# Low-rank products and key norms on exact halves, with two raw weight tiles in place of three, in a hybrid decoder layer

## The chip, the cores and the metric

The kernel runs on one core of a Trainium2 chip. What is measured is the device time of one execution, in microseconds (us). A core has five engines that run side by side and meet through semaphores: TensorE (PE; its weight loads are listed as PEld), VectorE (DVE), ScalarE (ACT), GpSimd (POOL) and SyncE (SP). Here SP issues nearly all of the transfers between memory and the on-chip buffer, one after the other; an issue whose conditions aren't met holds up those behind it.

## The reference

One layer of a decoder with a residual stream x of 512 tokens and 2048 features, in float32. One input projection of the normed x feeds three mixers, whose outputs are joined, projected and added to x; a SwiGLU feed-forward part (FFN) with 5632 hidden features and a last norm follow. The change lies in the third mixer, RWKV-7, which has 16 heads of 64 features:

```python
logw = -softplus(-(w0 + tanh(wl) @ w2)) - 0.5
decay = exp(-exp(logw))
a = sigmoid(a0 + al @ a2)                    # the "rate"
kk = k * k_k
kk = kk / max(sqrt(sum(kk * kk, per head)), 1e-12)
k = k * (1 + (a - 1) * k_a)
# then, per head and token t, with a state S of 64 x 64:
#   S = S * decay_t + (S @ -kk_t) (kk_t a_t)^T + v_t k_t^T ;  y_t = S @ r_t
```

`wl` and `al` are low-rank features (96 wide) that come out of the input projection, as r, k and v do.

## The kernel before

**Products.** All large products run on exact halves: an fp32 matrix w is split into wh = fp32r(w) and wl = w − wh, and a product takes three passes, wh·xh, wh·xl and wl·xh (`dense_k`, L237), all added up in one PSUM bank. A weight tile is 128x1024 (eight blocks of 128x128): one transfer into a `raw` tile issued on SP (L226), the cast to `wh` on ACT (L230), the subtraction to `wl` on DVE (L231), then 24 matmuls on PE, each 512 columns wide. There are three raw tiles and two pairs of `wh`, `wl`. Weights of the next projection are asked for before the current one runs (`sequence`). A few small products run on plain fp32 operands, where a matmul is two instructions.

**Stages.** `load_x` loads x, splits it and computes the low-rank features (pd_l). Then come the projections of the mixers, in this order: gl, then k, r, v of eight RWKV pairs (two heads each, numbered 0 to 7), then q, k, v of the attention heads (qa, ka, va, qb and so on). The output projection and the FFN follow.

**RWKV steps of a pair**, written as Python generators that stand in lanes: `rates` makes z (decay, from w2 and wl) and pa (rate, from a2 and al), each one fp32 product of 512 columns; `prep` makes kn (sums of squared keys per head, a product with the block-ones constant `onesbd`), then two halves of the score blocks gr, each of which DVE masks; `inverse` and `join` invert the unit triangular blocks: linv goes out to memory (li), comes back as x, is solved in a row of small DVE operations (xt, xy), goes out as xi and comes back into linv with four transfers on SP, and then three groups of 32x32 products on PE (px, pt, po) finish it. `chain` is the recurrence over eight chunks of 64 tokens: z on PE, a copy zs on ACT, u on PE, copies uv on ACT, S on PE, an update of uv on DVE, then the next z. `post` makes vt, bon, var and g. In names like z3_6 the first number is the pair, the second the chunk; z3 alone is the decay product. All the steps of several pairs overlap.

**What sets the order.** After each dense matmul a planner, `pump`, lets those lanes take a step whose time has come. It counts time by the matmuls issued: n/2400 + 0.013 us for an fp32r product of n columns, twice n/1200 for an fp32 one (`mm`), and an estimate for each ACT and DVE instruction. `need(name)` runs lanes, without dense matmuls, until the step named is done: the eviction of a projection needs the tile of the pair before to be free (pd_v of pair hp needs step v of pair hp − 1, pd_r needs that of hp − 2), and each attention projection needs some step of pair 7. On every engine the instructions run in the order so written.

Of the kernel before, what the change touches and what calls it, by code (L numbers as in the profile page):

```python
# [14 lines left out]
P = 128  # L15
T = 512
# [31 lines left out]
CST = {}  # L48
_n = 0
for _name, _w in (  # L50
    ("ident", 128), ("onesbd", 128), ("ones", 128), ("centre", 128), ("mask", 128),
    ("eps", 1), ("gneps", 1), ("kneps", 1), ("knmin", 1),
):
    CST[_name] = _n
    _n += _w
# [33 lines left out]
class Kernel:  # L89
# [178 lines left out]
    def run(self):  # L268
        nc, tc = self.nc, self.tc
        with contextlib.ExitStack() as es:  # L270
            enter = es.enter_context
            nc.push_inst_callback(self.charge)
            es.callback(nc.pop_inst_callback)
            self.cp = enter(tc.tile_pool(name="cp", bufs=1))
            self.raw = enter(tc.tile_pool(name="raw", bufs=3))
            self.hl = enter(tc.tile_pool(name="hl", bufs=2))
            self.pools = {"raw": [self.raw], "hl": [self.hl]}
            self.xp = enter(tc.tile_pool(name="xp", bufs=KT))
            self.dp = enter(tc.tile_pool(name="dp", bufs=1, space=bass.MemoryType.DRAM))
            self.pd = enter(tc.tile_pool(name="pd", bufs=2, space=bass.MemoryType.PSUM))  # L280
            self.pm = enter(tc.tile_pool(name="pm", bufs=2, space=bass.MemoryType.PSUM))

            self.cols = self.cp.tile([P, NCOL], F32, name="cols")
            self.cc = self.cp.tile([P, NCST], F32, name="cc")
            nc.scalar.dma_start(out=self.cols, in_=self.i["cols"])
            nc.scalar.preload_act_table_set("natural_log_exp_and_others")
            mixer = enter(contextlib.ExitStack())
            self.py = mixer.enter_context(tc.tile_pool(name="py", bufs=1, space=bass.MemoryType.PSUM))
            self.pc = mixer.enter_context(tc.tile_pool(name="pc", bufs=3, space=bass.MemoryType.PSUM))
            self.lora_ps = self.load_x()  # L290
            items = self.mixer_items(mixer.enter_context)

            def mixers_end():
                mixer.close()
                self.ffn_pools(enter)
            self.mixers_end = mixers_end
            y = []
            items += self.wout_items(y)
            items += self.ffn_items(y)
            self.sequence(items)  # L300

    def load_x(self):
# [3 lines left out]
        with self.tc.tile_pool(name="sx", bufs=KT) as sx:  # L306
# [5 lines left out]
            for q in range(4):  # L312
                for e in range(4):
                    k = 4 * q + e
                    xk = sx.tile([P, T], F32, tag="x", name=f"x{k}", bufs=KT)
                    nc.sync.dma_start(out=xk, in_=self.i["xT"][:, k, :])
                    hi = self.xp.tile([P, T], F32R, tag="xh", name=f"xh{k}")
                    lo = self.xp.tile([P, T], F32R, tag="xl", name=f"xl{k}")
                    g = self.col("g_attn", k)
                    nc.scalar.activation(hi, xk, AF.Copy, scale=g)  # L320
                    nc.vector.scalar_tensor_tensor(out=lo, in0=xk, scalar=g, in1=hi.bitcast(F32),
                                                   op0=ALU.mult, op1=ALU.subtract)
                    self.xr.append((hi, lo))
                    xs.append(xk)
                    if e < 3:
                        src, m = srcs[e]
                        raw = self.raw.tile([P, 4 * m], F32, tag="raw", name=f"raw_l{e}_{q}")
                        nc.sync.dma_start(out=raw.rearrange("p (k m) -> p k m", m=m), in_=src[:, 4 * q:4 * q + 4, :])
                        w = slice(4 * q * m, 4 * (q + 1) * m)
                        if q:  # L330
                            nc.gpsimd.tensor_copy(out=his[e][:, w], in_=raw)
                        else:
                            nc.scalar.copy(out=his[e][:, w], in_=raw)
                        nc.vector.tensor_tensor(out=los[e][:, w], in0=raw, in1=his[e][:, w].bitcast(F32),
                                                op=ALU.subtract)
            nc.scalar.dma_start(out=self.cc, in_=self.i["cst"])
            ps = [p.tile([P, T], F32, tag=t, name=f"pd_l{j}")
                  for j, (p, t) in enumerate(((self.pd, "d"), (self.pd, "d"), (self.pm, "m")))]
            for k in range(KT):
# [38 lines left out]
    def shift_steps(self, f, ps, mu, name, m=P):  # L378

        nc = self.nc  # L380
        h = self.rp.tile([P, T + 8], F32, tag="h", name=f"h_{name}", bufs=2)
        nc.gpsimd.memset(h[:m, 7:8], 0.0)
        nc.vector.tensor_tensor(out=h[:m, 8:], in0=ps[:m, :], in1=self.rstd1[:m, :], op=ALU.mult)
        yield
# [16 lines left out]
    def mixer_items(self, enter):  # L401
# [6 lines left out]
        nc.vector.tensor_scalar(out=self.ol, in0=self.cols[:, c0:c0 + n], scalar1=-1.0, scalar2=1.0,  # L408
                                op0=ALU.mult, op1=ALU.add)

        self.wl = lp.tile([97, T], F32, name="wl")
        nc.gpsimd.memset(self.wl[96:97, :], 1.0)
        f = rp.tile([P, T], F32, tag="r", name="f_wl", bufs=2)
        self.shifted(f, self.lora_ps[0], ("mu_wl", 0), "wl", 96)
        th = nc.scalar.activation(self.wl[:96, :], f[:96, :], AF.Tanh)
        with tc.issue_after(th.ins):
            nc.scalar.preload_act_table_set("natural_log_exp_and_others")
        self.al = lp.tile([P, T], F32, name="al")
        self.shifted(self.al, self.lora_ps[1], ("mu_al", 0), "al", 96)
        self.gl = []  # L420
        items = []
        for j in range(2):
            def go(ps, j=j):
                f = rp.tile([P, T], F32, tag="r", name=f"f_gl{j}", bufs=2)
                self.shifted(f, ps, ("mu_gl", j), f"gl{j}")
                g = lp.tile([P, T], F32, name=f"sgl{j}")
                self.sigmoid(g, f)
                self.gl.append(g)
            if j:
                items.append(self.proj(1, "gl1", go, (self.pc, "c")))  # L430
            else:
# [47 lines left out]
    def rates(self, hp):  # L479
        nc, rp = self.nc, self.rp  # L480
        q = self.in_flight[hp]
        if hp and f"prep{hp - 1}" not in self.done:
            yield lambda: not (hp and f"prep{hp - 1}" not in self.done)
        yield 1.0 if hp else 15.0
        ch = slice(hp * P, (hp + 1) * P)
        w2 = rp.tile([97, P], F32, tag="w2", name=f"w2_{hp}", bufs=3)
        a2 = rp.tile([96, P], F32, tag="w2", name=f"a2_{hp}", bufs=3)
        nc.sync.dma_start(out=w2, in_=self.i["w2"][:, ch])
        nc.sync.dma_start(out=a2, in_=self.i["a2"][:, ch])

        ps = self.pm.tile([P, T], F32, tag="m", name=f"z{hp}")
        self.mm(ps, w2, self.wl)
        sg = rp.tile([P, NCH, 65], F32, tag="rn", name=f"sg{hp}")
        nc.gpsimd.memset(sg[:, :, 0:1], 0.0)

        pa = self.pm.tile([P, T], F32, tag="m", name=f"pa{hp}")
        self.mm(pa, a2, self.al[:96, :], start=True, stop=True)
        a = rp.tile([P, T], F32, tag="a", name=f"a{hp}")
        self.sigmoid(sg[:, :, 1:65], ps.rearrange("p (n c) -> p n c", c=C))
        self.sigmoid(a, pa, nbias=self.na0[:, hp:hp + 1])  # L500
# [14 lines left out]
    def prep(self, hp):  # L515
# [7 lines left out]
        rn = rp.tile([P, T], F32, tag="rn", name=f"rn{hp}")  # L523
        kk_g = self.col("k_k", hp)
        nc.scalar.activation(rn, k, AF.Square, scale=kk_g)
        yield
        ps = self.pm.tile([P, T], F32, tag="m", name=f"kn{hp}")
        self.mm(ps, self.cst("onesbd", P), rn, start=True, stop=True)
        kk = rp.tile([P, T], F32, tag="kk", name=f"kk{hp}")
        with self.tc.high_priority(self.lead):  # L530

# [95 lines left out]
        rkm = rp.tile([P, P], F32, tag="w2", name=f"rkm{hp}", bufs=3)  # L627
        nc.scalar.activation(rkm, self.cst("onesbd", P), AF.Copy, scale=self.col("r_k", hp))
# [136 lines left out]
    def post(self, q, py):  # L765
# [7 lines left out]
        self.mm(ps, self.cst("onesbd", P), sq, start=True, stop=True)  # L773
# [103 lines left out]
    def diff_head(self, h, q, vtag):  # L877
        nc, rp = self.nc, self.rp
        if "setup" not in self.done:
            yield lambda: not ("setup" not in self.done)  # L880
        bias = rp.tile([P, T], F32, tag="h", name=f"bias{h}", bufs=2)
# [79 lines left out]
    def swa_tile(self, i, q, kv):  # L961

        nc, rp = self.nc, self.rp
        bias = rp.tile([P, 2, 256], F32, tag="h", name=f"biasb{i}", bufs=2)
# [148 lines left out]
    def ffn_pools(self, enter):  # L1113
# [3 lines left out]
        self.pf = enter(tc.tile_pool(name="pf", bufs=4, space=bass.MemoryType.PSUM))  # L1117
        self.acc2 = self.fp.tile([P, T], F32, name="acc2", bufs=1)
        self.xr2 = []
        raw = enter(tc.tile_pool(name="raw2", bufs=3))  # L1120
        hl = enter(tc.tile_pool(name="hl2", bufs=1))
        self.pools = {"raw": [self.raw, raw], "hl": [self.hl, self.hl, hl]}

# [192 lines left out]
```

## Time and profile before

| | us |
|---|---|
| median of 3 runs (lowest, highest) | 2424.39 (2423.8, 2425.11) |
| the profiled execution, its span | 2425.95, 2424.2 |
| start: x and the low-rank products | 0 to 46.6 |
| mixers, with the first half of the output projection | 46.6 to 859.9 |
| second half of the output projection | 859.9 to 965 |
| FFN | 965 to 2388 |
| last norm and output | 2388 to 2424.2 |

The profile gives for every group of instructions its busy time, the mean length of one, and the idle time before it with what ended it. The chain of waits follows the work back from the last instruction and splits the span by what it waited for. A stretch of the timeline gives start, length, engine, line and operation; matmuls overlap, so that the distance between two starts, not the length, is what one costs. Windows give the busy time of each engine between two points of time, and then the clock that TensorE was granted, as a share of full speed.

### The profile page before, as it was taken

The page shows a single profiled execution, that of the slowest core. Times are in us where ns is not written, and L with a number is a line of the kernel's source. Part 1 is how long each engine was busy: PE and PEld are TensorE (multiplying, and loading weights), DVE is VectorE, ACT ScalarE, POOL GpSimd, SP SyncE. Part 2 cuts the span into 40 slices and gives each one's busy share as a digit, 9 for nine tenths or more (in the row PEclk, how much of TensorE's full clock was granted, in tenths as well). Part 3 has the DMA queues.
Part 4 walks back from the last instruction along what each step waited for, and adds up shares of the span by engine and source line. Part 5 has one row for each costly group of instructions (what it writes and reads, how often), then busy time and mean ns, then how long its engine had stood idle before and what let it go on. Part 6 is the DMA issues. An engine that isn't in the chain of part 4 may idle for free.

```text
span 2424.2 us, 30859 instructions
## 1 busy us (share of the span) xinstructions
PE 2398.7 (99%) x12328; PEld 1912.3 (79%) x12328; DVE 1185.3 (49%) x2129; ACT 806.4 (33%) x1375; POOL 100.0 (4%) x158
## 2 busy tenths in 40 slices
PE   8999999999999999999999999999999999999997
PEld 6777767777777788888888888888888888888887
DVE  7578778664555544343343434343434333343437
ACT  5445554544444433222222222222222222222124
POOL 3000000000000013000000000000000000000007
PEclk9999999999999999999999999999999999999999
DMA  5322222223225233233222223222222322222333
GB/s 176 100 85 73 84 77 85 79 87 97 92 79 165 87 133 99 95 100 96 96 96 96 96 99 100 97 96 96 96 96 99 101 96 96 96 96 96 99 101 132
DMA packets 103794, 240.05 MB, mean 99 GB/s; under 512 B 34906, under 2 KB 43746, under 8 KB 103650
## 3 DMA queue, kind: packets, MB, share of 16 engines
q1 hardware_dynamic: 98754, 231.39, 29.9%
q10 hardware_dynamic: 4896, 6.69, 0.8%
q8 instruction: 97, 1.59, 0.3%
q14 instruction: 47, 0.39, 0.0%
HBM read 227.55 MB, written 10.49 MB: 98 GB/s over the span
## 4 chain that ended last, share of the span: by engine, by line
PE 92%; DVE 4%; DMA 1%; issue 1%; ACT 1%; POOL 0%; SPq 0%; DVEq 0%; ACTq 0%; POOLq 0%
PE pg L134 20%; PE pu L134 20%; PE pd L134 19%; PE po L134 8%; PE pd_r L134 3%; PE pd_v L134 3%; PE pd_k L134 2%; PE pd_ka L134 2%; PE pd_qa L134 2%; PE pd_va L134 2%; PE pd_qb L134 2%; PE pd_l L134 1%; PE z L134 1%; PE y L134 1%; DVE xy L659 1%
## 5 line engine op out<-in xcount | busy, mean ns | idle before, releaser
L134 PE MATMUL pd<-al,wh_wd 128*128 128x512 f32 (+1 forms) x768 | 285.3, 371 | 0.6 <-DVE al L1166 0.6
L134 PE MATMUL pd<-ah,wh_wd 128*128 128x512 f32 (+1 forms) x768 | 285.4, 372 | 0.4 <-DVE y L1185 0.4
L134 PE MATMUL pd<-ah,wl_wd 128*128 128x512 f32 (+1 forms) x768 | 285.2, 371 | 0.0
L134 PE MATMUL pu<-x1h,wh_wu 128*128 128x512 f32 x704 | 274.3, 390 | 0.0
L134 PE MATMUL pu<-x1h,wl_wu 128*128 128x512 f32 x704 | 273.9, 389 | 0.0
L134 PE MATMUL pu<-x1l,wh_wu 128*128 128x512 f32 x704 | 273.9, 389 | 0.0
L134 PE MATMUL pg<-x1h,wl_wg 128*128 128x512 f32 x704 | 273.9, 389 | 0.0
L134 PE MATMUL pg<-x1h,wh_wg 128*128 128x512 f32 x704 | 273.9, 389 | 0.0
L134 PE MATMUL pg<-x1l,wh_wg 128*128 128x512 f32 x704 | 273.9, 389 | 0.0
L1185 DVE TENSOR_TENSOR y<-y,pd 128x512 f32<-128x512 f32 (+1 forms) x192 | 122.6, 642 | 207.3 <-PE pd L134 207.1
L230 ACT CAST wh_wd<-raw_wd 128x1024 fp32r<-128x1024 f32 x96 | 101.0, 1052 | 356.9 <-PE pd L134 176.9
L230 ACT CAST wh_wu<-raw_wu 128x1024 fp32r<-128x1024 f32 x88 | 92.7, 1053 | 367.0 <-PE pu L134 144.7
L230 ACT CAST wh_wg<-raw_wg 128x1024 fp32r<-128x1024 f32 x88 | 92.7, 1054 | 362.5 <-PE pg L134 144.9
L231 DVE TENSOR_TENSOR wl_wg<-raw_wg,wh_wg 128x1024 fp32r<-128x1024 f32 x88 | 107.8, 1225 | 171.1 <-ACT wh_wg L230 171.1
L231 DVE TENSOR_TENSOR wl_wu<-raw_wu,wh_wu 128x1024 fp32r<-128x1024 f32 x88 | 107.8, 1225 | 133.4 <-ACT wh_wu L230 133.4
L134 PEld LDWEIGHTS pd<-al,wh_wd 128*128 128x128 f32 x768 | 144.6, 188 | 25.8 <-DVE al L1166 0.8
L134 PEld LDWEIGHTS pd<-ah,wh_wd 128*128 128x128 f32 x768 | 144.6, 188 | 25.5 <-issue 0.5
L134 PEld LDWEIGHTS pd<-ah,wl_wd 128*128 128x128 f32 x768 | 144.6, 188 | 24.9
L134 PEld LDWEIGHTS pu<-x1l,wh_wu 128*128 128x128 f32 x704 | 132.1, 188 | 27.7 <-issue 0.2
L134 PEld LDWEIGHTS pu<-x1h,wh_wu 128*128 128x128 f32 x704 | 132.1, 188 | 27.6 <-issue 0.2
L134 PEld LDWEIGHTS pu<-x1h,wl_wu 128*128 128x128 f32 x704 | 132.1, 188 | 27.5
L134 PEld LDWEIGHTS pg<-x1h,wl_wg 128*128 128x128 f32 x704 | 132.1, 188 | 27.5
(356 smaller groups left out, 4070.0 us busy)
## 6 DMA issues: line engine op xcount, KB each, us to landing
raw_wd<-in_w_down SPq DMA_DIRECT2D x96, 512.0 KB, 3.2
raw_wg<-in_w_gate SPq DMA_DIRECT2D x88, 512.0 KB, 3.8
raw_wu<-in_w_up SPq DMA_DIRECT2D x88, 512.0 KB, 3.7
raw_wo<-in_w_out SPq DMA_DIRECT2D x32, 512.0 KB, 3.3
raw_k<-in_w_in SPq DMA_DIRECT2D x16, 512.0 KB, 3.9
raw_r<-in_w_in SPq DMA_DIRECT2D x16, 512.0 KB, 3.9
raw_v<-in_w_in SPq DMA_DIRECT2D x16, 512.0 KB, 3.8
x<-in_xT SPq DMA_DIRECT2D x16, 256.0 KB, 5.0
```

The lines of the kernel that those rows point to most:

```text
L134: self.tc.keep_in_program_order(self.nc.tensor.matmul(out, lhsT, rhs, start=start, stop=stop))
L230: nc.scalar.copy(out=hi[:, :kn * m], in_=s)
L231: nc.vector.tensor_tensor(out=lo[:, :kn * m], in0=s, in1=hi[:, :kn * m].bitcast(F32), op=ALU.subtract)
L659: nc.vector.tensor_tensor(out=y[:, 0:m, j + 1:32], in0=y[:, 0:m, j + 1:32], in1=tmp[:, :m, :n], op=ALU.add)
L1185: nc.vector.tensor_tensor(out=o, in0=o, in1=ps, op=ALU.add)
```

## The change

The decay and rate products z and pa become three passes on halves each: `wl` and `al` are split once at the start, w2 and a2 of a pair are loaded into one tile `wa`, now asked for before the wait for the preceding pair, and split into `wah` and `wal` by two casts on ACT and two subtractions on DVE. kn becomes two passes: the squares are split into `sqk` (one cast, one subtraction), the block-ones constant is exact in fp32r and is kept as `blk`, loaded later and apart from the other constants. To make room, the mixers have two raw weight tiles in place of three (the small low-rank weights at the start get a pool of their own, with three), the tile `h` of the token shift one in place of two. The FFN's second raw pool has four tiles in place of three, so the FFN has six in all, as before.

```diff
             self.cp = enter(tc.tile_pool(name="cp", bufs=1))
-            self.raw = enter(tc.tile_pool(name="raw", bufs=3))
+            self.raw = enter(tc.tile_pool(name="raw", bufs=2))
...
-                        raw = self.raw.tile([P, 4 * m], F32, tag="raw", name=f"raw_l{e}_{q}")
+                        raw = sx.tile([P, 4 * P], F32, tag="raw", name=f"raw_l{e}_{q}", bufs=3)[:, :4 * m]
...
-        h = self.rp.tile([P, T + 8], F32, tag="h", name=f"h_{name}", bufs=2)
+        h = self.rp.tile([P, T + 8], F32, tag="h", name=f"h_{name}")
...
+    def halves(self, pool, src, name):
+
+        hi, lo = (pool.tile([P, src.free_size()], F32R, name=name + e)[:src.shape[0], :] for e in "hl")
+        self.nc.scalar.copy(out=hi, in_=src)
+        self.nc.vector.tensor_tensor(out=lo, in0=src, in1=hi.bitcast(F32), op=ALU.subtract)
+        return hi, lo
...
+        self.wl, self.al = (self.halves(lp, z[:n, :], name) for z, n, name in ((wl, 97, "wl"), (al, 96, "al")))
...
+        blk = rp.tile([P, P], F32, tag="rkm", name="blkr")
+        nc.scalar.dma_start(out=blk, in_=self.i["cst"][:, CST["onesbd"]:])
+        self.blk = lp.tile([P, P], F32R, name="blk")
+        nc.scalar.copy(out=self.blk, in_=blk)
...
     def rates(self, hp):
...
+        ch = slice(hp * P, (hp + 1) * P)
+        wa = rp.tile([97, 2, P], F32, tag="wa", name=f"wa{hp}")
+        nc.sync.dma_start(out=wa[:, 0, :], in_=self.i["w2"][:, ch])
+        nc.sync.dma_start(out=wa[:96, 1, :], in_=self.i["a2"][:, ch])
         if hp and f"prep{hp - 1}" not in self.done:
             yield lambda: not (hp and f"prep{hp - 1}" not in self.done)
-        yield 1.0 if hp else 15.0
...
+        if not hp:
+            yield 15.0
+        wah = rp.tile([97, 2, P], F32R, tag="wah", name=f"wah{hp}")
+        wal = rp.tile([97, 2, P], F32R, tag="wal", name=f"wal{hp}")
+        for e, n in ((0, 97), (1, 96)):
+            w, hi, lo = (t[:n, e, :] for t in (wa, wah, wal))
+            nc.scalar.copy(out=hi, in_=w)
+            nc.vector.tensor_tensor(out=lo, in0=w, in1=hi.bitcast(F32), op=ALU.subtract)
+        yield
+
+        def three(ps, e, n, x):
+            for i, (w, y) in enumerate(((wah, 0), (wah, 1), (wal, 0))):
+                self.mm(ps, w[:n, e, :], x[y], start=(i == 0), stop=(i == 2))
+
...
-        self.mm(ps, w2, self.wl)
+        three(ps, 0, 97, self.wl)
...
-        self.mm(pa, a2, self.al[:96, :], start=True, stop=True)
+        three(pa, 1, 96, self.al)
...
+        sq = rp.tile([P, 2, T], F32R, tag="bk", name=f"sqk{hp}")
+        nc.scalar.copy(out=sq[:, 0, :], in_=rn)
+        nc.vector.tensor_tensor(out=sq[:, 1, :], in0=rn, in1=sq[:, 0, :].bitcast(F32), op=ALU.subtract)
         yield
         ps = self.pm.tile([P, T], F32, tag="m", name=f"kn{hp}")
-        self.mm(ps, self.cst("onesbd", P), rn, start=True, stop=True)
+        for e in range(2):
+            self.mm(ps, self.blk, sq[:, e, :], start=(e == 0), stop=(e == 1))
...
-        raw = enter(tc.tile_pool(name="raw2", bufs=3))
+        raw = enter(tc.tile_pool(name="raw2", bufs=4))
```

The planner counts the shorter products, and the pools have other depths, so the written order moves on all engines. Three places follow. Rows give line, operation, output<-inputs and shape; the last number of a name is the tile's own.

The first place is SP's queue around the transfers that bring the inverse of pair 6 back (linv0<-xi6). raw_ka0_8 is the second half of the weights of projection ka0, and so on. Before:

```order
L226 DMA raw_ka0_8_4795<-in_w_in 128x1024
L674 DMA linv0_481<-xi6_4746 32x8x32 x4
L226 DMA raw_va0_0_4963<-in_w_in 128x1024
L226 DMA raw_va0_8_4969<-in_w_in 128x1024
L226 DMA raw_qa1_0_5276<-in_w_in 128x1024
L596 DMA li7_5097<-linv1_482 32x8x32 x4
L852 DMA dist_5725<-in_dist 128x768
L650 DMA x_5148<-li7_5097 32x1024 x4
L717 DMA g2_6_5234<-in_g2 128x2x128
L226 DMA raw_qa1_8_5282<-in_w_in 128x1024
```

And now:

```order
L226 DMA raw_va0_0_5129<-in_w_in 128x1024
L226 DMA raw_va0_8_5135<-in_w_in 128x1024
L881 DMA dist_5895<-in_dist 128x768
L746 DMA g2_6_5371<-in_g2 128x2x128
L226 DMA raw_qa1_0_5273<-in_w_in 128x1024
L692 DMA xi6_5094<-xy_4725 256x1x32 x4
L488 DMA mix13_5177<-ysq5_5145 128x512
L226 DMA raw_qa1_8_5279<-in_w_in 128x1024
L703 DMA linv0_493<-xi6_5094 32x8x32 x4
L625 DMA li7_5266<-linv1_494 32x8x32 x4
L679 DMA x_5351<-li7_5266 32x1024 x4
```

The transfers linv0<-xi6 stood behind raw_ka0_8, and now stand behind raw_va0_0, raw_va0_8, raw_qa1_0 and raw_qa1_8.

The second place is TensorE around px of pair 6 (the products on linv0) and the score blocks gr of pair 7. Before, from the end of the first half of gr7:

```order
L134 MATMUL pd_ka0_4975<-xh1_106,wl_ka0_0_4792 128x512
L134 MATMUL z5_5_5005<-uv5_3856,Z5_3640 64x64 x2
L134 MATMUL y5_4769<-Z5_3640,uv5_3856 64x64 x2
L134 MATMUL px_5014<-cc_76,linv0_481 32x32 x16
L134 MATMUL pd_ka0_4975<-xh2_116,wh_ka0_0_4791 128x512
L134 MATMUL u5_5_5035<-zs5_5_5008,linv2_483 128x64
L134 MATMUL pd_ka0_4975<-xl2_117,wh_ka0_0_4791 128x512
...
L134 MATMUL pt_5051<-xnn_5031,linv0_481 32x32 x16
L134 MATMUL pd_ka0_4975<-xh4_132,wh_ka0_0_4791 128x512
...
L134 MATMUL gr7_1_0_5081<-Z7_4934,bk7_4837 128x128
L134 MATMUL gr7_1_1_5082<-Z7_4934,bk7_4837 128x128
```

And now, from the end of pd_ka0 (gr7_0 is the first half of the score blocks, gr7_1 the second; a row "..." leaves out more of the same half):

```order
L134 MATMUL pd_ka0_5141<-xh15_234,wh_ka0_8_4939 128x512
L134 MATMUL pd_ka0_5141<-xl15_235,wh_ka0_8_4939 128x512
L134 MATMUL pd_ka0_5141<-xh15_234,wl_ka0_8_4940 128x512
L134 MATMUL gr7_0_0_5214<-Z7_5184,bk7_5113 128x128
L134 MATMUL gr7_0_1_5215<-Z7_5184,bk7_5113 128x128
...
L134 MATMUL px_5230<-cc_76,linv0_493 32x32 x16
L134 MATMUL gr7_1_0_5250<-Z7_5184,bk7_5113 128x128
L134 MATMUL gr7_1_1_5251<-Z7_5184,bk7_5113 128x128
...
L134 MATMUL pd_va0_5285<-xh0_96,wh_va0_0_5131 128x512
L134 MATMUL pt_5287<-xnn_5247,linv0_493 32x32 x16
```

px had dense matmuls of pd_ka0 and steps of pair 5's recurrence around it; now it stands between the two halves of gr7, behind the last product of pd_ka0.

The third place is TensorE at chunk 6 of pair 3's recurrence. Before, at the end of pd_v5:

```order
L134 MATMUL z3_6_3631<-uv3_2647,Z3_2351 64x64 x2
L134 MATMUL y3_3340<-Z3_2351,uv3_2647 64x64 x2
L134 MATMUL pd_v5_3483<-xh15_234,wh_v5_8_3190 128x512
L134 MATMUL pd_v5_3483<-xl15_235,wh_v5_8_3190 128x512
L134 MATMUL pd_v5_3483<-xh15_234,wl_v5_8_3191 128x512
L134 MATMUL pd_k6_3664<-xh0_96,wh_k6_0_3473 128x512
L134 MATMUL u3_6_3666<-zs3_6_3634,linv0_481 128x64
L134 MATMUL pd_k6_3664<-xl0_97,wh_k6_0_3473 128x512
...
L134 MATMUL S3_6_3678<-uv3_2647,bkn3_2580 64x64 x2
L134 MATMUL y3_3340<-gr3_2356,uv3_2647 64x64 x2
```

And now, at the end of pd_v6:

```order
L134 MATMUL pd_v6_3820<-xh15_234,wh_v6_8_3683 128x512
L134 MATMUL pd_v6_3820<-xl15_235,wh_v6_8_3683 128x512
L134 MATMUL pd_v6_3820<-xh15_234,wl_v6_8_3684 128x512
L134 MATMUL z3_6_4050<-uv3_2874,Z3_2642 64x64 x2
L134 MATMUL y3_3740<-Z3_2642,uv3_2874 64x64 x2
L134 MATMUL pt_4059<-xnn_4025,linv1_494 32x32 x16
L134 MATMUL u3_6_4079<-zs3_6_4053,linv0_493 128x64
L134 MATMUL S3_6_4093<-uv3_2874,bkn3_2820 64x64 x2
L134 MATMUL y3_3740<-gr3_2647,uv3_2874 64x64 x2
L134 MATMUL po_4100<-linv1_494,pts_4076 32x32 x16
L138 MATMUL bt5_0_4120<-cc_76,bk5_3666 128x128 x4
L138 MATMUL bt5_1_4126<-cc_76,bk5_3666 128x128 x4
```

Between z3_6, u3_6 and S3_6 stood nine dense matmuls; now chunk 6 begins behind the last matmul of pd_v6 and no dense matmul stands between its steps or before chunk 7.

More of the change, by code (lines that the diff above doesn't have):

```diff
@@ L50 @@
 for _name, _w in (
-    ("ident", 128), ("onesbd", 128), ("ones", 128), ("centre", 128), ("mask", 128),
-    ("eps", 1), ("gneps", 1), ("kneps", 1), ("knmin", 1),
+    ("ident", 128), ("ones", 128), ("centre", 128), ("mask", 128),
+    ("eps", 1), ("gneps", 1), ("kneps", 1), ("knmin", 1), ("onesbd", 128),
 ):
@@ L283, in run @@
             self.cols = self.cp.tile([P, NCOL], F32, name="cols")
-            self.cc = self.cp.tile([P, NCST], F32, name="cc")
+            self.cc = self.cp.tile([P, CST["onesbd"]], F32, name="cc")
             nc.scalar.dma_start(out=self.cols, in_=self.i["cols"])
@@ L335, in load_x @@
                                                 op=ALU.subtract)
-            nc.scalar.dma_start(out=self.cc, in_=self.i["cst"])
+            nc.scalar.dma_start(out=self.cc, in_=self.i["cst"][:, :CST["onesbd"]])
             ps = [p.tile([P, T], F32, tag=t, name=f"pd_l{j}")
@@ L409, in mixer_items @@
                                 op0=ALU.mult, op1=ALU.add)
-        self.wl = lp.tile([97, T], F32, name="wl")
-        nc.gpsimd.memset(self.wl[96:97, :], 1.0)
+        wl = rp.tile([97, T], F32, tag="k", name="wl")
+        nc.gpsimd.memset(wl[96:97, :], 1.0)
         f = rp.tile([P, T], F32, tag="r", name="f_wl", bufs=2)
         self.shifted(f, self.lora_ps[0], ("mu_wl", 0), "wl", 96)
-        th = nc.scalar.activation(self.wl[:96, :], f[:96, :], AF.Tanh)
+        th = nc.scalar.activation(wl[:96, :], f[:96, :], AF.Tanh)
         with tc.issue_after(th.ins):
             nc.scalar.preload_act_table_set("natural_log_exp_and_others")
-        self.al = lp.tile([P, T], F32, name="al")
-        self.shifted(self.al, self.lora_ps[1], ("mu_al", 0), "al", 96)
+        al = rp.tile([P, T], F32, tag="v", name="al")
+        self.shifted(al, self.lora_ps[1], ("mu_al", 0), "al", 96)
+        self.wl, self.al = (self.halves(lp, z[:n, :], name) for z, n, name in ((wl, 97, "wl"), (al, 96, "al")))
         self.gl = []
@@ L481, in rates @@
         q = self.in_flight[hp]
+        ch = slice(hp * P, (hp + 1) * P)
+        wa = rp.tile([97, 2, P], F32, tag="wa", name=f"wa{hp}")
+        nc.sync.dma_start(out=wa[:, 0, :], in_=self.i["w2"][:, ch])
+        nc.sync.dma_start(out=wa[:96, 1, :], in_=self.i["a2"][:, ch])
         if hp and f"prep{hp - 1}" not in self.done:
             yield lambda: not (hp and f"prep{hp - 1}" not in self.done)
-        yield 1.0 if hp else 15.0
[L485 to L489, printed above, removed]
+        if not hp:
[10 more added lines that the diff above has]
+                self.mm(ps, w[:n, e, :], x[y], start=(i == 0), stop=(i == 2))
         ps = self.pm.tile([P, T], F32, tag="m", name=f"z{hp}")
-        self.mm(ps, w2, self.wl)
+        three(ps, 0, 97, self.wl)
         sg = rp.tile([P, NCH, 65], F32, tag="rn", name=f"sg{hp}")
@@ L626, in prep @@
         q["uv"] = uv
-        rkm = rp.tile([P, P], F32, tag="w2", name=f"rkm{hp}", bufs=3)
-        nc.scalar.activation(rkm, self.cst("onesbd", P), AF.Copy, scale=self.col("r_k", hp))
+        rkm = rp.tile([P, P], F32, tag="rkm", name=f"rkm{hp}")
+        nc.scalar.activation(rkm, self.blk.bitcast(F32), AF.Copy, scale=self.col("r_k", hp))
         ps = self.pm.tile([P, T], F32, tag="m", name=f"bon{hp}")
@@ L772, in post @@
         ps = self.pc.tile([P, T], F32, tag="c", name=f"var{hp}")
-        self.mm(ps, self.cst("onesbd", P), sq, start=True, stop=True)
+        self.mm(ps, self.blk.bitcast(F32), sq, start=True, stop=True)
         nc.scalar.activation(sq, ps, AF.Ln, bias=self.cst("gneps", 1), scale=1.0 / 64)
@@ L880, in diff_head @@
             yield lambda: not ("setup" not in self.done)
-        bias = rp.tile([P, T], F32, tag="h", name=f"bias{h}", bufs=2)
+        bias = rp.tile([P, T], F32, tag="h", name=f"bias{h}")
         nc.scalar.mul(out=bias, in_=self.dist, mul=DIFF_SLOPES[h])
@@ L963, in swa_tile @@
         nc, rp = self.nc, self.rp
-        bias = rp.tile([P, 2, 256], F32, tag="h", name=f"biasb{i}", bufs=2)
+        bias = rp.tile([P, 2, 256], F32, tag="h", name=f"biasb{i}")
         for c in range(2):
```

## The prediction

> **What bounds the kernel now.** I read the page first, then busy time by stage, then what TensorE waited for, and last the chain of waits.
>
> ```profile
> span 2424.2 us, 30859 instructions
> PE 2398.7 (99%) x12328; PEld 1912.3 (79%) x12328; DVE 1185.3 (49%) x2129; ACT 806.4 (33%) x1375; POOL 100.0 (4%) x158
> PE 92%; DVE 4%; DMA 1%; issue 1%; ACT 1%; POOL 0%; SPq 0%; DVEq 0%; ACTq 0%; POOLq 0%
> ```
>
> TensorE is busy 99% of the span and 92% of the chain. So a matmul that is removed shortens the kernel by its own length, and so does every microsecond in which TensorE is made to wait lengthen it. The stages (columns: length, then busy time of PE, PEld, DVE, ACT) show where there was anything left:
>
> ```profile
> 46.60:859.90 813.30, 809.45 (x5172) 595.14 (x5170) 516.83 (x1364) 393.51 (x882) 13.09 (x82) 1.00 0.30 91
> 965.00:2388.00 1423.00, 1422.45 (x6386) 1182.19 (x6385) 560.20 (x625) 337.49 (x379) 19.09 (x18) 1.00 0.30 98
> ```
>
> The mixers, where all of the edits lie, lose only 813.30 − 809.45 = 3.9 us. The list of what TensorE waited for names them (total, times, longest):
>
> ```profile
> PE gr L134 <- DVE gr L585: 1.6, 2, 0.8
> PE wt L138 <- DVE pa L906: 1.3, 2, 0.9
> PE z L134 <- DVE uv L754: 0.4, 1, 0.4
> ```
>
> No row names a wait of px, the first product of the block inverse, on a DMA, and the recurrence (z) loses 0.4 us in 64 chunks. This schedule is full. The change must therefore be read twice: what the shorter products give, and what the new order takes.
>
> **What the shorter products give.** Pieces of the chain (start, length, what):
>
> ```profile
> 1009.78 10.88 PE pg L134 x48
> 459.73 0.86 PE z L134 x2
> 460.59 0.86 PE pa L134 x2
> 230.24 0.86 PE kn L134 x2
> 474.07 1.05 PE kn L134 x2
> 95.84 1.09 PE gr L134 x16
> ```
>
> A 512-column pass on exact halves takes 10.88 / 48 = 0.227 us. An fp32 product is two instructions and 0.86 us. Per pair, z and pa become six passes: 1.72 − 1.36 = 0.36 us. kn becomes two: 0.86 − 0.45 = 0.41 (0.60 by the row with 1.05, which follows a short product and so holds some of that one's filling time). Times eight pairs: 0.77 × 8 = 6.2 us, at most 0.96 × 8 = 7.7; I take 6.2. The new passes have contractions of 97, 96 and 128 rows; that they run at the dense rate is read off the neighbouring dense matmuls, a lower bound of the gain being none at all if they kept 0.86.
>
> ACT and DVE get the splits. Their prices are those of casts and subtractions already there:
>
> ```profile
> L230 ACT CAST wh_wd<-raw_wd 128x1024 fp32r<-128x1024 f32 x96 | 101.0, 1052 | 356.9 <-PE pd L134 176.9
> L231 DVE TENSOR_TENSOR wl_wg<-raw_wg,wh_wg 128x1024 fp32r<-128x1024 f32 x88 | 107.8, 1225 | 171.1 <-ACT wh_wg L230 171.1
> 470.99 0.69 DVE L383 TENSOR_TENSOR h_v<-pd_v,rstd_a 128x512 f32<-128x512 f32 x1 [2.90 <-PE pd_v L134]
> 120.00:130.00 10.00, 10.00 (x44) 7.91 (x43) 9.25 (x33) 6.34 (x9) 0.10 (x1) 1.00 0.30 100
> ```
>
> Per pair the squares cost DVE one 128x512 subtraction, 0.69 us, and the rate weights two of 128 columns, about 0.3 each (an estimate: a fixed part and the slope between 0.69 at 512 and 1.23 at 1024 columns): 1.3 us; ACT about as much. Over the mixers DVE is busy 517 of 813 us, so the time hides behind TensorE nearly everywhere. It does not around pair 1, where DVE is busy 9.25 of 10 us and the masks on gr are already what TensorE waits for: there 1.3 to 1.9 us more on DVE, against 1.5 us less on TensorE, turns the gr wait of 1.6 into 2.1: +0.5. Covered elsewhere, uncovered it would be 8 × 1.3 = 10 us.
>
> **What the new order takes: the queue of SP.** The planner counts TensorE's products at their new lengths, so the RWKV steps fall 30 to 100 dense matmuls later against the projections. With two raw tiles in place of three, each weight load on SP waits for the subtraction of the tile two back, one tile (24 matmuls, 5.4 us) later than before. SP issues in order. In the order shown above, the four transfers linv<-xi of pair 6 stood behind raw_ka0_8; now they stand behind raw_va0_8, raw_qa1_0 and raw_qa1_8. SP before, with its issue times, and px:
>
> ```profile
> 469.53 0.55 SPq L226 DMA_DIRECT2D raw_ka<-in_w_in  x1
> 470.92 1.81 SPq L674 DMA_DIRECT2D linv<-xi  x4
> 472.87 0.35 SPq L226 DMA_DIRECT2D raw_va<-in_w_in  x1
> 492.73 0.69 PE L134 MATMUL px<-cc,linv 32*32 32x32 f32 x32
> DMA to landing us min/median/max: 1.8/2.8/4.4
> ```
>
> The last row is the transfer's landing time after its issue. So px had 492.73 − 470.92 = 21.8 us to spare. In the new order raw_qa1_8 takes the buffer of raw_va0_8, which is free when wl_va0_8 is done, which follows wh_va0_8, which takes the buffer that the last product of pd_ka0 reads. From that product the path is: cast 1.05, subtraction 1.23, raw issue 0.35, three linv issues 1.36, landing of the fourth 2.8, and hops between engines of about 0.5 (estimate): 7.3 us; between 6.3 and 8.9 with landings of 1.8 and 4.4. Between that product and px TensorE's order holds only the first half of gr7, the 1.09 us of the gr row above (eight products of two instructions), and no dense matmul. The stall is 6.2 us (5.2 to 7.8). Behind px stand the other half of gr7 and then the whole of pd_va0, so all of it shows. The mechanism falls only if the transfers could be issued past the waiting weight load.
>
> The same at **px of pair 2**: linv<-xi now stands behind raw_k5_8, where before it stood ahead of it. That load hangs by the same path on the end of pd_r4. Between lie seven dense matmuls (1.6) and half of gr3 (1.1): 7.3 − 2.7 = 4.6; as one of the hops may overlap I take 4.4 (3.4 to 6). px of pair 4 hangs on raw_r7_0 with 6.7 us of work between: 0.6 (0 to 2). The other five keep 11 us or more.
>
> **The recurrence.** A projection's eviction needs the previous pair's tile free, so where the lag has grown the planner lets the remaining steps run with no dense matmuls between them. In the order shown above this is chunks 6 and 7 of pair 3 at the end of pd_v6 and, shorter, chunks 3 and 4 of pair 4 at the end of pd_k7. What a step then waits for, in the rows of pair 5's first chunk:
>
> ```profile
> 469.04 0.33 PE L134 MATMUL z<-uv,Z 64*64 64x64 f32 x4
> 469.42 0.21 ACT L728 COPY zs<-z 128x64 f32<-128x64 f32 x1 [1.46 <-PE z L134]
> 470.34 0.33 PE L134 MATMUL u<-zs,linv 128*128 128x64 f32 x2
> 470.53 1.05 ACT L230 CAST wh_qa<-raw_qa 128x1024 fp32r<-128x1024 f32 x1 [0.90 <-PE pd_v L134]
> 471.49 0.44 ACT L743 COPY uv<-u 64x64 f32<-64x64 f32 x2
> 471.62 1.23 DVE L231 TENSOR_TENSOR wl_qa<-raw_qa,wh_qa 128x1024 fp32r<-128x1024 f32 x1
> 471.81 0.44 PE L134 MATMUL S<-uv,bkn 128*64 128x64 f32 x3
> 472.76 0.59 DVE L756 TENSOR_SCALAR uv<-S,D 64x64 f32<-64x64 f32 x2
> 473.48 0.34 PE L134 MATMUL z<-uv,Z 128*64 128x64 f32 x4
> ```
>
> z to z took 4.44 us, with the weight's cast ahead of the copy on ACT and its subtraction ahead of the update on DVE; dense matmuls filled all of it. At the end of pd_v6 a cast and a subtraction stand ahead in the same way, and the filling is bt, vt and the small products of the inverse. From z to u: two scalings and the cast ahead on ACT, then zs, against 0.9 us of y and pt between: 0.95 left. From u to S: copies of 0.44 and two hops, nothing between: 0.75. From S to the next z: h_v and wl (1.9) ahead on DVE, then 0.59, against po and bt: 0.5. Then z to u again, 0.75. That is 3.0 us there, and 1.7 at pd_k7 in the same way with one cast and one new subtraction (sqk) ahead. The parts of each hop are estimates from these rows, and the engines may run further ahead than I took, so the bounds are 0 and 4.7; I take the middle, 2.4.
>
> **The clock.** What a stall costs beyond itself is seen once in before:
>
> ```profile
> 147.21 0.46 PE L134 MATMUL gr<-Z,bk 64*128 64x128 f32 x2 [0.81 <-DVE gr L585]
> 148.43 1.13 PE L134 MATMUL gr<-Z,bk 64*128 64x128 f32 x14 [0.77 <-DVE gr L585]
> 149.87 0.63 PE L134 MATMUL pd_r<-xl,wh_r 128*128 128x512 f32 x1
> 153.23 0.39 PE L134 MATMUL pd_r<-xh,wh_r 128*128 128x512 f32 x1
> 150.00:160.00 10.00, 10.00 (x100) 7.92 (x98) 4.26 (x9) 2.63 (x5) 0.83 (x6) 0.84 0.36 83
> ```
>
> After 1.58 us of idle time in two pieces eight dense matmuls took 153.23 − 149.87 = 3.36 us in place of 1.81, and the granted clock of that stretch is 0.84: 1.55 us. I expect it again after px of pairs 6 and 2 and at the end of pd_v6: 3 × 1.55 = 4.7 (bounds: none, and 5 × 1.55 = 7.8).
>
> [...]
>
> **Sum.** Two waits go: wt on DVE (1.3), which now has 10 to 15 dense matmuls ahead in place of 6 to 14. The start issues the two first raw_gl loads before the last low-rank weights and has 64 KB less of constants to bring: 0 (−0.3 to +1.5). In the FFN depth four against three changes nothing, as it lost 0.5 us of 1423. In us: −6.2 − 1.3 + 0.5 + 6.2 + 4.4 + 0.6 + 2.4 + 4.7 = +11.3. The profiled execution took 2425.95 with a span of 2424.2; it lies 1.6 above the median of the runs, 2424.39, and the sum moves either alike. Against the median: 2435.7, say 2436.
>
> **Rivals.**
> *Nothing new waits.* The linv transfers land in time, because ACT and DVE run ahead of what I took (the last product of a tile is not what frees its buffers), and the chain's hops hide. For it: before has no wait of px at all. Against: the order has no dense matmuls there to hide 7.3 us. Time: 2424.4 − 6.2 − 1.3 + 0.5 = 2417.4, faster. It decides if the path is shorter than the work between, 1.1 and 2.7 us. Chance 0.13.
> *The stalls are there at their lower ends and the clock stays up*: −7.0 + 5.2 + 3.4 + 0 + 0 = +1.6, 2426, no difference. For it: small waits of 0.9, 0.6 and 0.4 us in before left the clock alone. Chance 0.17, with the cases in which only one of the two px stalls appears.
> *The whole chain stalls.* All hops open (4.7) and both px at their upper ends (7.8, 6, 2), clock 7.8: −7.0 + 28.3 = +21, 2446. For it: a delayed inverse pushes the next pair's steps against the same ends of projections. Chance 0.17.
> *The splits do not shorten the products* (a pass costs more at 97 rows, or the weight loads show): the stalls without the gain, 2442. Against it: 96-row passes run in the low-rank products at the start. Chance 0.03.
> My forecast has 0.50.
>
> **Numbers.** What a measurement of this kernel can tell from no change is about 0.2%, 4.8 us: 2419.5 to 2429.2. Faster 0.13; same 0.17; slower 0.70. For the forecast alone the range is 2429 to 2443 (landing times, hops and clock at their bounds, not all at once). The range of 8 in 10 runs from 2419 to 2447: it leaves out most of the first rival and the tail of the third.
>
> **What would show it.** The list of TensorE's waits should have a new row, px on a DMA, with two or three entries and a longest of about 6 us, while wt's goes. z and pa should read six passes of 0.227 in 1.36 us. The chain's DMA share should rise from 1%. Windows around these two places should show a granted clock under 1. If px has no row, the queue argument is wrong, and the kernel should be faster by 6 us or more; if px waits but the total is under 2429, the stalls were sized too high or the clock did not drop.

## The result

The changed kernel is slower: 2455.06 us in the median of 4 runs (2454.08 to 2456.25) against 2424.75 before, ratio 1.0125 [1.0113, 1.0137], 30 us more. The forecast had the sign, slower, but its 2436, its range up to 2443 and its wide range up to 2447 were all too low. The profiled execution took 2454.22 us with a span of 2452.1, 27.9 longer than before's.

TensorE's waits after (total, times, longest; the rows that the change touches), to be held against the same list of before:

```profile
PE px L134 <- DMA linv<-xi: 14.3, 6, 5.7
PE pd_l L134 <- ACT hl L333: 6.8, 2, 5.6
PE pd_l L134 <- DVE ll L334: 2.3, 1, 2.3
PE S L134 <- ACT uv L772: 2.2, 4, 0.8
PE pd_r L134 <- DVE wl_r L231: 1.5, 1, 1.5
PE pt L134 <- ACT xnn L714: 1.4, 1, 1.4
PE z L134 <- DVE uv L783: 1.0, 2, 0.6
PE wt L138 <- DVE pa L935: 0.3, 1, 0.3
```

px on a DMA is new and the largest, as forecast, though in four pairs and not in two or three. The forecast's other sign, a larger DMA share in the chain of waits, can't be read: the chain of after goes back only to 657 us, behind all of this. In the timeline px waits in pairs 1 (2.05 and 0.56), 2 (4.04), 4 (1.65 and 0.27) and 6 (5.74). The stretch in which the loss arises, first before, then after (length, busy time of PE, PEld, DVE, ACT, POOL, then the granted clock):

```profile
150.00:600.00 450.00, 449.36 (x3411) 319.70 (x3409) 306.82 (x846) 233.78 (x562) 7.35 (x56) 1.00 0.29 82
```

```profile
150.00:600.00 450.00, 430.40 (x3217) 311.96 (x3217) 302.82 (x833) 222.33 (x528) 7.34 (x56) 0.95 0.27 76
```

TensorE was idle 19.6 us in place of 0.6, and the mean clock was 0.95 in place of 1.00. The clock around px of pairs 1 and 6, in stretches of 3.41 us:

```profile
217.25:220.66 3.41, 3.12 (x47) 2.83 (x47) 0.80 (x3) 0.72 (x2) 0.10 (x1) 0.50 0.50 159
220.66:224.08 3.42, 3.42 (x37) 2.46 (x38) 2.42 (x6) 0.36 (x1) 0.00 (x0) 0.50 0.50 122
224.08:227.49 3.41, 3.41 (x18) 2.23 (x18) 0.00 (x0) 0.36 (x1) 0.00 (x0) 0.50 0.54 153
531.28:534.69 3.41, 0.96 (x28) 0.89 (x30) 0.17 (x1) 0.00 (x0) 0.00 (x0) 0.50 0.45 108
534.69:538.10 3.41, 3.41 (x44) 2.68 (x41) 0.98 (x3) 0.72 (x2) 0.00 (x0) 0.50 0.00 0
538.10:541.52 3.42, 3.42 (x33) 2.78 (x28) 1.46 (x4) 0.73 (x2) 0.00 (x0) 0.50 0.21 34
541.52:544.93 3.41, 3.41 (x49) 2.79 (x48) 0.00 (x0) 1.21 (x3) 0.00 (x0) 1.00 0.45 112
```

At either place the clock is at half for three such stretches, the last two without any idle time in them. Over the mixers the half-clock stretches are 41.0 us long in all (six places: 10.2, 6.8, 3.4, 3.4, 6.8 and 10.2) against 3.4 before. If half of what isn't idle in them counts as lost (an estimate), that is 17.9 us against 1.7. With the idle time of the mixers (22.1 against 3.9) and the products, which cost 1.40 in place of 1.73 us (z and pa) and 0.47 in place of 0.88 (kn) from start to start where dense products stand around them, the account is

+18.3 (idle) + 16.2 (clock, the estimate) − 5.9 (products, 8 × 0.74) = +28.6 us, and the spans differ by 27.9.

So the gain is there, and it is lost almost six times over. The question is what makes px wait. The forecast's theory is the *queue theory*: linv<-xi stands behind weight loads on SP, which wait longer with two raw tiles. The trace after suggests another, the *solve theory*. The timeline of DVE, ACT, SP and PE at px of pair 6, rows left out between:

```profile
524.10 0.17 DVE L688 TENSOR_TENSOR xy<-xy,xt 128x8 f32<-128x8 f32 x1
...
524.98 2.56 SPq L692 DMA_DIRECT2D xi<-xy  x4
...
526.72 1.04 ACT L230 CAST wh_va<-raw_va 128x1024 fp32r<-128x1024 f32 x1 [4.01 <-PE pd_ka L134]
526.84 1.16 PE L134 MATMUL gr<-Z,bk 64*128 64x128 f32 x16
...
527.64 0.55 SPq L488 DMA_DIRECT2D mix<-ysq  x1
527.79 1.23 DVE L231 TENSOR_TENSOR wl_va<-raw_va,wh_va 128x1024 fp32r<-128x1024 f32 x1 [0.16 <-ACT wh_va L230]
...
529.05 0.34 SPq L226 DMA_DIRECT2D raw_qa<-in_w_in  x1
...
529.56 1.81 SPq L703 DMA_DIRECT2D linv<-xi  x4
...
533.73 1.30 PE L134 MATMUL px<-cc,linv 32*32 32x32 f32 x32 [5.74 <-DMA linv<-xi]
```

raw_qa1_8 does go out the moment wl_va is done (529.02), as the queue theory says. But the triangular solve on DVE had ended only at 524.27, and its result must go out as xi and come back: the last of xi's four transfers was issued at 526.93, and linv<-xi can't go out before it has landed. In pairs 0, 2, 3, 4, 5 and 7 linv<-xi followed that last issue by 1.9 to 2.1 us; here by 2.6. So the queue cost about 0.5 us. For px of pair 2 the load left at 279.63 and linv<-xi at 281.07, when xi (issued 276.96 to 279.54) had landed: there the queue cost nothing. From the solve's end to px's start lay 6.5, 7.6, 7.9 and 9.5 us in the four pairs, the first wait included; without it TensorE would have come to px 4.5, 3.6, 6.3 and 3.7 us after the solve. In before it came 7.5 us or more after it, in all eight pairs.

### The profile page after: what moved, and what is told of

Read it like the earlier page. It is cut to its first block, busy times and chain, and to the rows that moved or that the text cites. A ratio compares the mean times of both kernels' runs of the same rounds, so it can differ in the third digit from the quotient of the medians.

```text
span 2452.1 us, 30935 instructions
## 1 busy us (share of the span) xinstructions
PE 2406.4 (98%) x12344; PEld 1924.4 (78%) x12344; DVE 1192.4 (49%) x2155; ACT 814.7 (33%) x1402; POOL 100.2 (4%) x158
## 4 chain that ended last, share of the span: by engine, by line
PE 72%; POOL 0%; DVE 0%; issue 0%; ACT 0%; DVEq 0%; ACTq 0%; POOLq 0%
PE pg L134 20%; PE pu L134 20%; PE pd L134 19%; PE po L134 7%; PE pd_qb L134 2%; PE pd_ka L134 1%; PE pd_va L134 1%; PE pd_qa L134 1%; PE sb L134 0%; PE sa L134 0%; PE ob L134 0%; PE oa L134 0%; POOL acc L1160 0%; PE wtb L138 0%; DVE y L1258 0%
## 5 line engine op out<-in xcount | busy, mean ns | idle before, releaser
L134 PEld LDWEIGHTS pg<-x1l,wh_wg 128*128 128x128 f32 x704 | 132.1, 188 | 27.5
```

The lines of the kernel that those rows point to most:

```text
L134: self.tc.keep_in_program_order(self.nc.tensor.matmul(out, lhsT, rhs, start=start, stop=stop))
```

## The experiments

**Two raw tiles alone.** The kernel before with the weight pools of the change (the diff leaves out the start's own pool), no new work; the written order is unchanged.

```diff
-            self.raw = enter(tc.tile_pool(name="raw", bufs=3))
+            self.raw = enter(tc.tile_pool(name="raw", bufs=2))
...
-        raw = enter(tc.tile_pool(name="raw2", bufs=3))
+        raw = enter(tc.tile_pool(name="raw2", bufs=4))
```

> The kernel before with two raw weight tiles in the mixers (four instead of three in the FFN's second pool, the start's own three), nothing else; the written order of every engine stays as it was. Queue theory (the forecast's): the weight loads hold up SP one tile longer, but in the old order px had 7.5 us or more between the product that frees the load and itself, so px waits at most 1 us: 2424 to 2427 us. Solve theory (px waits because the triangular solve on DVE ends late against TensorE's written order): raw depth plays no part, 2424 to 2425 us, no wait of px. Rival, depth by itself: with two tiles the weights come late at the ends of projections (in after, pd_r waited 1.5 us for wl_r once): 2428 us or more.

Measured: 2424.91 against 2424.91, ratio 1.000 [0.999, 1.001], and no wait of px. The rival of depth by itself falls. The queue and the solve theory had both allowed for this.

**linv<-xi on another queue.** The changed kernel, `join`:

```diff
         for h, b, bl in blocks:
-            nc.sync.dma_start(out=L[bl, :, bl], in_=d[h, b].rearrange("n i g t -> (i g) n t"))
+            nc.gpsimd.dma_start(out=L[bl, :, bl], in_=d[h, b].rearrange("n i g t -> (i g) n t"))
```

> The changed kernel with the four transfers linv<-xi issued on POOL's queue in place of SP's. Queue theory: they no longer stand behind weight loads, px's waits (14.3 us) fall below 4 us and with them much of the half clock: 2432 to 2440 us. Solve theory: the transfers can't start before the solve has gone out as xi and landed, which the trace of after shows 1.5 us or less ahead of their issue; px still waits 11 us or more, 2450 to 2457 us.

Measured: 2459.0, ratio 1.0143 [1.0128, 1.0158]. Two rows of its waits:

```profile
PE px L134 <- DMA linv<-xi: 12.5, 6, 5.2
PE px L134 <- POOL xy L676: 4.0, 1, 4.0
```

px waits 16.5 us in all. Freed of SP's queue, the transfers went out 2.5 to 3.0 us behind the last issue of xi in the four pairs, against 2.1 to 2.6 in after, and took longer to land (median 3.1 us against 2.1). POOL's queue is thus not a clean substitute, but the queue theory asked for 10 us less and there is nothing of it. It falls as the cause of the four waits; the 0.5 us of pair 6 stay with it.

**The old order with all the new work.** `unseen` makes the planner's charge and clock pass over the new instructions; z, pa and kn are counted as before. Every product then stands where it stood among the dense matmuls (z 72, 260, 423 and so on; kn of pair 0 one later). Shown is h1, in which the squares' split has priority on its engines; in h3 it hasn't. kn is treated as z and pa are.

```diff
-        if eng not in self.free or not ins.outs or not hasattr(ins.outs[0], "ap"):
+        if self.unseen or eng not in self.free or not ins.outs or not hasattr(ins.outs[0], "ap"):
...
-        if lhsT.dtype == F32R:
+        if self.unseen:
+            pass
+        elif lhsT.dtype == F32R:
...
-        if hp and f"prep{hp - 1}" not in self.done:
-            yield lambda: not (hp and f"prep{hp - 1}" not in self.done)
-        if not hp:
-            yield 15.0
         wah = rp.tile([97, 2, P], F32R, tag="wah", name=f"wah{hp}")
         wal = rp.tile([97, 2, P], F32R, tag="wal", name=f"wal{hp}")
+        self.unseen = True
         for e, n in ((0, 97), (1, 96)):
...
-        yield
+        self.unseen = False
+        if hp and f"prep{hp - 1}" not in self.done:
+            yield lambda: not (hp and f"prep{hp - 1}" not in self.done)
+        yield 1.0 if hp else 15.0
...
+            self.unseen = False
+            self.now += 2 * T / 1200
...
-        nc.scalar.copy(out=sq[:, 0, :], in_=rn)
-        nc.vector.tensor_tensor(out=sq[:, 1, :], in0=rn, in1=sq[:, 0, :].bitcast(F32), op=ALU.subtract)
+        self.unseen = True
+        with self.tc.high_priority():
+            nc.scalar.copy(out=sq[:, 0, :], in_=rn)
+            nc.vector.tensor_tensor(out=sq[:, 1, :], in0=rn, in1=sq[:, 0, :].bitcast(F32), op=ALU.subtract)
+        self.unseen = False
...
```

> The changed kernel with the planner's clock kept blind to the new instructions (z, pa and kn charged as the fp32 products they replace, the splits not at all; the rate weights' split at the start of a pair's rates, the squares' split with priority on its engines): every product stands at the same place among the dense matmuls as in before, with two raw tiles and all the new work on ACT and DVE. Order theory (the loss comes from where the steps now stand): px's waits go, half clock falls to 3 to 7 us, and the shorter products show less up to 3 us of waits for the splits: 2418 to 2424 us. Work theory (the loss comes from 2 x 1.3 us more of ACT and DVE work per pair, which makes the solve and the masks late wherever they stand): px waits 5 us or more in all, 2432 us or more.

> As h1, but the squares' split without priority, so it stands in ACT's and DVE's order where it was written. Order theory: kn waits for sqk behind a weight tile's subtraction (1.2 us) in some pairs, up to 6 us in all: 2420 to 2428 us. Work theory: 2432 us or more, as h1.

Measured: h1 2425.06, ratio 1.0006 [0.9996, 1.0015]; h3 2424.78, ratio 1.0004 [0.9994, 1.0013]. The order theory's side: all of the loss of 30 us is gone with two raw tiles, one tile `h` and all the new work still there; the work theory (2432 or more) falls. h1 is a microsecond over its range and little is left of the products' gain, since in h3

```profile
PE px L137 <- DMA linv<-xi: 3.0, 2, 2.6
PE gr L137 <- DVE xy L703: 1.2, 1, 1.2
PE wt L141 <- DVE pa L950: 1.1, 2, 0.7
```

px of pair 0 waits 3.0 us: the solve of pair 0 ended at 149.3 in place of 146.6, behind DVE's new work, and px stands where it stood. That the squares' split has priority (h1) or not (h3) makes no difference to be measured; kn waited for nothing of note in either.

**px later.** As h3, `join` with 3 us more ahead of px:

```diff
-        yield 10.0
+        yield 13.0
```

> As h3, with 3 us more of planned time between the issue of linv<-xi and px, in all pairs: px stands 7 to 35 dense products later behind gr than in h3, save for pairs 4 and 5 (201 and 172 against 217 and 223). Solve theory: no wait of px, the gain of the shorter products (8 x 0.74 = 5.9 us, as h3's trace has it) shows for the most part: 2418 to 2421 us, faster than before. Rival (the products' gain is eaten by something that the waits don't name): 2423 us or more.

Measured: 2420.09, ratio 0.9983 [0.9974, 0.9993], faster than before. px has no row in the list of waits. The time lies in the solve theory's range.

**The products' lengths counted, the splits not.** As h3, without the corrections to `self.now`, so that `mm` charges the new passes itself.

```diff
-            self.now += 2 * T / 1200
...
-        self.now += 2 * T / 1200
```

> As h3, but the planner counts z, pa and kn at their new, shorter lengths (0.68 and 0.45 us against 1.7 and 0.85 per pair); the splits stay unseen. The written order then moves by 2 to 90 dense products. Order theory: px stands 149 and 161 dense products behind gr of pairs 2 and 5, where before had 170 and 223, and waits there again: 2425 to 2438 us. Splits theory (it is the splits that the planner counts, not the lengths, that spoil the order): 2418 to 2424 us.

Measured: 2419.29, ratio 0.9978 [0.9968, 0.9987], the lowest median of all: the expectation read from the distances failed. px of pairs 2 and 5 stood 149 and 161 dense products behind gr but did not wait, since the solve of pair 2 took 25.6 us here (214.6 to 240.2) against 39.9 in after (236.7 to 276.6). So a distance counted in dense products from gr doesn't tell when a solve ends. The splits theory has it right for this kernel.

**The rate weights' split counted.** As h3, with the charge for the four instructions.

```diff
     def rates(self, hp):
-        self.unseen = True
         for e, n in ((0, 97), (1, 96)):
```

> As h3, but the planner counts the split of the rate weights (two casts, two subtractions) at the start of each pair's rates; the order moves by about 10 dense products, and px of pair 0, which waited 3.0 us in h3, stands 12 dense products (2.7 us) later. Order theory: px of pair 0 waits less than 1 us, px of pair 6, 147 behind its gr in place of 169, may wait 2 us: 2420 to 2425 us.

Measured: 2429.62, ratio 1.0019 [1.0009, 1.0029]. px of pair 0 waits no more, but that of pair 6 does, longer than expected:

```profile
PE px L137 <- DMA linv<-xi: 4.3, 1, 4.3
PE z L137 <- DVE uv L799: 1.3, 1, 1.3
PE gr L137 <- DVE xt L701: 1.2, 1, 1.2
```

Four small instructions in the planner's account moved the steps by some 10 dense products and cost some 4 us against h3 (1.0019 against 1.0004; the fastest run here, 2427.76, is slower than the slowest of h3, 2427.34).

**Idle time filled.** The changed kernel, with unused dense products ahead of px:

```diff
+        fill = {1: 12, 2: 18, 4: 8, 6: 26}.get(hp, 0)
+        if fill:
+            pf, now = self.pc.tile([P, T], F32, tag="c", name=f"fill{hp}"), self.now
+            for j in range(fill):
+                self.mm(pf, self.xr[0][0][:, :P], self.xr[j % KT][0], start=(j == 0), stop=(j == fill - 1))
+            self.now = now
         ps = self.pc.tile([P, NCH, 32], F32, tag="c", name="px")
```

> The changed kernel with idle dense products put before px of pairs 1, 2, 4 and 6 (12, 18, 8 and 26 of 512 columns, results unused, not counted by the planner): 64 x 0.227 = 14.5 us of work in the place of px's 14.3 us of waits, so that the waits cost the same but TensorE is busy in them. Wait theory (the half clock follows TensorE's idle time): the half-clock windows behind px go, of 17.9 us that they cost some 5 remain, 2440 to 2446 us. Small-product theory (the clock drops because px, pt and the 64-row products load the array little, idle or not): 2452 to 2457 us.

Measured: 2443.22, ratio 1.0081 [1.0066, 1.0096]; 11 us less than after by the ratios, with 14.5 us of work added (15.2 from the first of the 64 products to px, in the four places together). The two stretches behind px of pair 6, and the stretch of the loss:

```profile
528.90:532.30 3.40, 3.40 (x44) 2.62 (x44) 1.40 (x4) 0.73 (x2) 0.00 (x0) 1.00 0.24 39
532.30:535.70 3.40, 3.40 (x28) 2.69 (x22) 0.00 (x0) 1.92 (x5) 0.00 (x0) 1.00 0.51 158
150.00:600.00 450.00, 443.94 (x3365) 322.63 (x3363) 308.95 (x852) 226.95 (x540) 7.45 (x57) 1.00 0.26 79
```

Full clock with the same small products (1.00 in both, where after has 0.50 in the three stretches around and behind this px): here half clock went with the idle time and not with the products. One stretch of 3.4 us is left in the mixers; the mean clock of the execution was 0.998, as in before, against 0.990 in after. TensorE's order is that of after but for the 64 products, so the traces can be held against each other: from the first product of gl to the first of the FFN after took 947.5 us and the filled kernel 934.6. So 11 (by the medians) to 13 us (by these two traces) of the 30 are shown to be clock, less than the estimate of 16.2, and the wait theory's range holds.

**One yield.** The changed kernel without the bare yield behind the weights' split. A bare yield makes the step wait for the planner's estimate of when DVE has worked off its backlog.

```diff
             nc.vector.tensor_tensor(out=lo, in0=w, in1=hi.bitcast(F32), op=ALU.subtract)
-        yield
 
         def three(ps, e, n, x):
```

> The changed kernel without the one bare yield behind the split of the rate weights (a bare yield makes the step wait for the planner's estimate of DVE's backlog): z of pair 0 stands 72 dense products into the mixers as in before, not 126, and the other steps 10 to 60 earlier than in after. Order theory: px stands 146 dense products or more behind gr, so px waits in one pair (5) and by 3 us or so; but the last six steps of pair 7's chain now stand with no dense products between: 2428 to 2446 us. Rival (the new work on ACT and DVE is what costs): no change, 2450 us or more.

Measured: 2433.7, ratio 1.0038 [1.0025, 1.0051]: 21 of the 30 us are gone with this line. px waits nowhere, not even in pair 5, where 3 us were expected; there are other waits in its place, at the end of the last chain among them:

```profile
PE u L134 <- ACT zs L756: 2.8, 2, 2.1
PE pa L134 <- ACT sg L404: 1.4, 2, 0.7
PE gr L134 <- DVE xy L687: 1.3, 1, 1.3
PE var L134 <- ACT ysq L798: 0.7, 1, 0.7
```

**One part alone.** The squares alone (`rates` as before), and the low-rank products alone (kn one fp32 product on `rn`), each with two raw tiles.

> The change without its low-rank part: z and pa stay fp32 products, only kn runs on split squares; two raw weight tiles; the planner counts all of it. Saving 8 x 0.41 = 3.3 us. Order theory: the order moves by up to 80 dense products, px of pair 2 stands 141 behind gr (before: 170) and waits some 3 us with a half-clock window behind it: 2421 to 2432 us. If the order were indifferent: 2421 us.

> The change without its squares: z and pa in three passes, kn an fp32 product as before; two raw weight tiles; the planner counts all of it. Saving 8 x 0.33 = 2.6 us. Order theory: z of pair 0 stands 126 dense products in as in after; px of pairs 1, 4 and 6 stands 149 to 156 behind gr, with steps of the chain of pair 5 unfilled: 2428 to 2450 us. If the squares' part made the loss: 2422 us.

Measured: s_sq 2435.74, ratio 1.0047 [1.0033, 1.0062]; s_lora 2439.02, ratio 1.0063 [1.0046, 1.008]. Each part alone saves TensorE time and costs 12 and 15 us. px again, in one pair each, 2 and 1:

```profile
PE px L134 <- DMA linv<-xi: 7.9, 2, 7.3
```

```profile
PE px L134 <- DMA linv<-xi: 5.5, 2, 5.0
```

s_sq's place was expected (pair 2), its size, 3 us, was not: 7.9, and its time lies over its range. There TensorE came to px half a microsecond before the solve had even ended (265.8 against 266.3). In s_lora pairs 1, 4 and 6 were expected to wait, and only pair 1 did.

## Why the prediction was wrong

- **Products**: forecast −6.2; the trace has 8 × 0.74 = −5.9. Right.
- **Two raw tiles**: by the forecast px had 21.8 us to spare in the old order, and the two tiles made it wait in the new one. The first was right (b_raw2); the second fell. The step that failed is that of "the queue of SP": the path from the last product of pd_ka0 through wl to linv<-xi is real (7.0 us from the cast at 526.72 to px at 533.73; 7.3 were forecast, of which 0.5 for hops was an estimate that named no row; the trace has 0.03 from cast to subtraction, 0.03 to the weight load and 0.17 to linv<-xi), but it ended only about 0.5 us later than the other path, from the end of the solve through xi. I had worked out only the former. For pair 6 the two happen to be nearly equal, so 6.2 us were forecast and 5.7 came. For pair 2, 4.4 were forecast and 4.0 came, by luck: the queue cost nothing there. In pairs 1 and 4 only the solve was late; I had 0 (pair 1 was to keep 11 us or more) and 0.6, and 2.6 and 1.9 came.
- **Masks of pair 1**: gr +0.5 forecast; gr's wait (1.6) went, and pd_r waited 1.5 for wl_r in about the same place. The sum, 2.1 against 1.5, is off by 0.6 us, and the form was another.
- **wt** fell from 1.3 to 0.3; it was forecast to go.
- **Recurrence**: 2.4 forecast, 0 to 4.7; S, z and y waited 3.5 against 0.4. At the end of pd_v6 it is 1.05 of the 3.0, at pd_k7 0.9 of the 1.7; the rest stands elsewhere. pt's 1.4 was not forecast.
- **Clock**: the term that was mis-sized most. Forecast 3 × 1.55 = 4.7, bounds 0 to 7.8; the account has 16.2, and the filled kernel shows 11 to 13. Three stretches of 3.4 us were forecast, one per stall, because before's only case had one; twelve came. The three places that were forecast (px of pairs 6 and 2, the end of pd_v6) had seven, and the other five stood in places that were not: px of pair 1 (three), px of pair 4, pt. By the account the clock is 11.5 of the 16.6 us between the forecast's +11.3 and the spans' +27.9; most of the rest are the stalls of pairs 1 and 4, pt and the recurrence. What keeps the clock down in the later stretches, which have no idle time, was not tested. In before and after the 13 half-clock stretches of the mixers part by what TensorE did in them: all five with five or more products of 512 columns were the last of their place, five of the six with three or fewer were followed by another, and of the two with four one was. In the filled kernel, without the idle time, the clock was 1.00 over the same small products. Before has one stretch of 3.41 us, with eight products of 512 columns in it; behind px of pairs 1 and 6 in after the clock stayed at half for one more such stretch after one without idle time.
- **Rivals**: "the whole chain stalls" gave 2446 and was the nearest; its clock term, 7.8, was still half of the account's.

Behind all of it stands what was named only as a premise: the written order moved. h1 and h3 show that the same work in the old order costs nothing, and p1 and h3k that in another it is faster by 4 to 5 us. Of h3's gain of 5.9 us its waits explain 2.6; the spans of h3 and before differ by 1.8, so some 1.5 us of it aren't found; the runs of h3 spread over 3.2 us.

## What to carry to other kernels

When a hand-made or planned order decides what runs between two waits, read a change first as a change of that order: a yield and a few charges were worth 30 us here, five times the arithmetic saved. For each transfer that is consumed soon after it lands, follow every path to it and not only the one that the change seems to touch; px had two, of nearly one length. And price a stall with the half clock that the traces show behind it: here, filling 14 us of idle time with useless products brought 11 us.

## What was not expected

Half clock lasted up to 10.24 us behind one stall (px of pair 1 and of pair 6 in after), with no idle time in its last 6.8 us. It followed idle time that could be shorter than one of its stretches: in before and in after the clock changed only at multiples of 3.41 us from its first change, and of the full-clock stretches of the mixers on this grid, in the two traces, 4 had 1.6 us or more of idle time and all were followed by half clock, 3 had 1.0 to 1.6 us and two were (1.57 in either kernel; 1.54 was not), 12 had 0.25 to 1.0 us and one was (0.76, itself behind a half-clock stretch), and 441 had less and none was. A solve of the same 62 small operations took from 20 to 44 us (s_sq pair 7: 536.4 to 556.2; before pair 4: 338.0 to 382.2); between them DVE does other work.
